# B, C and x of a state space mixer: from 256-channel to 512-channel products, with PE transposes behind them

## The chip, the cores and the metric

The kernel runs on one core of a Trainium2 chip. The metric is device time in microseconds (us): 1674.48 us is the median of three runs of the kernel before (1671.82 to 1675.09). TensorE (PE) does matmuls, VectorE (DVE) and ScalarE (ACT) work element by element, GpSimd (POOL) does almost nothing here, and SyncE (SP) issues the loads. PE writes to PSUM, of which this kernel uses two pools of four one-bank tiles each.

## The reference, cut to what matters

One encoder block: 256 tokens of width 2048 are normed, multiplied by one wide input matrix, and the columns are given to two mixers side by side (a Mamba-2 state space mixer, SSD, and an RWKV-7 mixer). Their outputs go through one output matrix, and a gated feed-forward part follows. All is float32. The change touches the columns `xbc` of the state space mixer:

```python
u = rms_norm(h, norm1_g[l])
P = u @ w_in[l]                       # 256 x 11744
xbc = P[..., o1:o2]                   # 2048 columns x, 512 columns B, 512 columns C
xbc = jax.nn.silu(causal_depthwise_conv(xbc, conv_w, conv_b))   # 4 taps along the tokens, per channel
xs = xbc[..., :D_SSD]
Bm = xbc[..., D_SSD:D_SSD + 512].reshape(b, s, 4, 128)          # four groups
Cm = xbc[..., D_SSD + 512:].reshape(b, s, 4, 128)
```

The convolution runs along the tokens and has its own weights for each channel.

## The kernel before

**Products.** Every matrix of weights comes from memory as "raw" tiles of 128 partitions x 1024 float32 (512 KB). `split` (L189) makes two halves of each: `whi`, rounded by ACT (L192), and `wlo = raw - whi`, by DVE (L193). The activations are kept split in the same way (`uh`, `ul`). Each product is the sum of three matmuls: high x high, high x low, low x high. One raw tile, with its two halves, is called a unit here. There are four buffers each for `raw`, `whi` and `wlo`, so a raw tile is loaded when the `wlo` of the unit four before it has been made, and a `whi` is made when PE has done with the unit four before it.

There are two forms of product:

- `gemm_a` (L267) puts channels on the partitions: the weights are the stationary operand (128 x 128), and the 256 tokens stream past. It makes 256 channels in one PSUM tile with 16 x 2 x 3 = 96 matmuls of 256 columns, 24 to a unit. The norm's factor of each token then lies along the columns, and `scaled` (L229, its instruction is L231) multiplies it in on DVE.
- `gemm_b` (L284) puts tokens on the partitions: the activations are stationary (two halves of 128 tokens), and 512 columns of weights stream past. It makes 512 channels in two PSUM tiles with 16 x 2 x 3 = 96 matmuls of 512 columns, 12 to a unit. The norm's factor of a token is then one number per partition, which an ACT instruction can take as its scale.

**The state space mixer.** B and C (L934 to L944): four `gemm_a` of 256 channels, each followed by `scaled` and two `conv`. A `conv` (L928) of 128 channels is one ACT instruction (L930) and three DVE instructions (L932) that read the product from PSUM; it needs channels on the partitions, since its weights are per channel. One Silu over all of B and C ends it. Then, for each of the four groups g (L1054 on): first a part of the output product of the RWKV mixer (g = 0 and 1); two `gemm_a` of 256 channels for x, each with `scaled`, two `conv` and a Silu into `xc`; for g = 2 and 3 a part of the output product of this mixer (`add_out`, which calls `gemm_b`); then the gate z as one `gemm_b`, with two ACT instructions that take it out of PSUM (L1072); then the group's scan as ten steps (`ssd_group`).

**What sets the order.** Small work is interleaved with the products by hand: `Side` (L42) is a queue of functions with due times in ticks, and the products call `side.tick(0.5)`; a unit is one tick in either form. The tail of the RWKV mixer (a chain of small dependent steps) is spread over the B and C products in this way, and its last pair over group 0; the scan of group g over the products behind it. A scheduler then orders each engine's instructions by a simulation, with the order of the program as priority; it also gives tiles their buffers. All loads are issued by SP in one queue.

Of the kernel before, what the change touches and what calls it, by code (L numbers as in the profile page):

```python
# [10 lines left out]
F32 = mybir.dt.float32  # L11
F32R = mybir.dt.float32r
AF = mybir.ActivationFunctionType
# [3 lines left out]
P = 128  # L17
T = 256
D = 2048
KT = D // P  # L20
D_FF = 5632
CXBC = 2048
# [46 lines left out]
def tile_hybrid_block(ctx: ExitStack, tc: tile.TileContext, x, norm1_g, w_in, conv_w, conv_b, dt_bias, A_log, D_skip,  # L69
                      ssd_norm_g, mu, w0, w2, a0, a2, g2, k_k, k_a, r_k, gn_w, gn_b, w_out, norm2_g, w_gate, w_up,  # L70
                      w_down, norm_f_g, out):
    nc = tc.nc
    PS = bass.MemoryType.PSUM
    x = x[0]
    out = out[0]
    w_in, conv_w, w2, a2, g2 = w_in[0], conv_w[0], w2[0], a2[0], g2[0]
# [4 lines left out]
    wpool = ctx.enter_context(tc.tile_pool(name="wpool", bufs=3))  # L81
# [4 lines left out]
    side = Side()  # L86

    def mmt(name):
        return mm.tile([P, 2, T], F32, name=name, tag="mm")

    def mxt(name):
        return mx.tile([P, 512], F32, name=name, tag="mx")
# [7 lines left out]
    ident = const.tile([P, P], F32, name="ident")  # L100
# [13 lines left out]
    ps = mxt("ps_up")  # L114
# [9 lines left out]
    rows = [init.tile([P, P], F32, name=f"rows{i}") for i in range(3)]  # L124
# [27 lines left out]
    for hh in range(2):  # L152
        for s in range(2):
            m = mask2[hh * 64:(hh + 1) * 64, s]
# [4 lines left out]
    for s in range(2):  # L159
        for hh in range(2):  # L160
            a = hh * 64
# [20 lines left out]
    ps = mxt("ps_cols")  # L182
# [13 lines left out]
    uh = ul = R = None  # L196
    ssq = [const.tile([P, 2, 4], F32, name=f"ssq{i}") for i in range(3)]
    rstd = [const.tile([P, 2], F32, name=f"rstd{i}") for i in range(3)]
# [30 lines left out]
    def scaled(ps):  # L229

        nc.vector.tensor_tensor(ps, ps, R.unsqueeze(1).broadcast_to([P, 2, T]), ALU.mult)  # L231
        return ps
# [34 lines left out]
    def gemm_a(w, cols, name, units=None):  # L267
        ps = mmt(name)
        for k0 in range(0, KT, 4):
            hi, lo = split(load_a(w, cols, k0)) if units is None else units(k0 // 4)  # L270
            for k in range(4):
                kt = k0 + k
                first, last = kt == 0, kt == KT - 1
                for b in range(2):
                    o = ps[:, b]
                    wh, wl = hi[:, k, b * P:(b + 1) * P], lo[:, k, b * P:(b + 1) * P]
                    nc.tensor.matmul(o, wh, uh[:, kt], start=first and b == 0, stop=False)  # L277
                    nc.tensor.matmul(o, wh, ul[:, kt], start=False, stop=False)  # L278
                    nc.tensor.matmul(o, wl, uh[:, kt], start=False, stop=last and b == 1)  # L279
                if k % 2:  # L280
                    side.tick(0.5)
        return ps

    def gemm_b(w, r0, c0, acts, name, turned=False):  # L284


        ps = [mmt(name).rearrange("p a t -> p (a t)") for _ in range(2)]
        n = len(acts)
        wv = w[r0:r0 + n * P, c0:c0 + 512].rearrange("(k p) c -> p k c", p=P)
        for k0 in range(0, n, 2):  # L290
            raw = wpool.tile([P, 2, 512], F32, name="raw", tag="raw", bufs=4)
            if turned:
                nc.sync.dma_start(out=raw[:, 0], in_=wv[:, k0])
                for a in range(2):
                    nc.sync.dma_start(out=raw[a * 64:a * 64 + 64, 1], in_=wv[64 - a * 64:P - a * 64, k0 + 1])
            else:
                nc.sync.dma_start(out=raw, in_=wv[:, k0:k0 + 2])
            hi, lo = split(raw)
            for k in range(2):
                kt = k0 + k  # L300
                first, last = kt == 0, kt == n - 1
                ah, al = acts[kt]
                for b in range(2):
                    s = slice(b * P, (b + 1) * P)
                    nc.tensor.matmul(ps[b], ah[:, s], hi[:, k], start=first, stop=False)  # L305
                    nc.tensor.matmul(ps[b], ah[:, s], lo[:, k], start=False, stop=False)  # L306
                    nc.tensor.matmul(ps[b], al[:, s], hi[:, k], start=False, stop=last)  # L307
                side.tick(0.5)
        return ps

    def add_out(w, r0, ys, then=None, turned=False, ns=range(4)):

# [30 lines left out]
    for r, c in ((rows[1], colB), (rows[0], colA), (rows[2], colC)):  # L343
        ps = mxt("ps_cols")
# [27 lines left out]
    pst = ExitStack()  # L372
    pp = pst.enter_context(tc.tile_pool(name="pp", bufs=1, side="right"))

    ps = scaled(ps_l0)
# [4 lines left out]
    ps = scaled(gemm_a(w_in, [(0, 96, CWD), (96, 32, CDT), (128, 128, CAD)], "ps_l1"))  # L380
# [501 lines left out]
    def window(pi, ticks):  # L882
        if pi < 8:
            w = pairs[pi]
            w["load"]()
            for t, n in zip(PREP, ("decay", "rate", "keys", "keys2", "keysum", "btt", "vt", "ktt")):
                side.at(t, w[n])
        if 0 < pi < 9:
            w = pairs[pi - 1]
            for t, f in zip(AMATS, w["amats"]):  # L890
                side.at(t, f)
            for t, f in zip(INV, w["inv"]):
                side.at(t if ticks >= 16 else t * (ticks - 0.5) / 16, f)
        if pi > 1:
            for t, f in zip(CHAIN, pairs[pi - 2]["chain"]):
                side.at(t if ticks >= 16 else t * (ticks - 0.5) / 16, f)
# [11 lines left out]
    for pi in range(8):  # L908
# [3 lines left out]
        for i, (n, c) in enumerate((("k", CK), ("v", CV), ("r", CR))):  # L912
            ps = scaled(gemm_a(w_in, [(0, 256, c + pi * 256)], "ps_rkv"))
            t = pp.tile([P, 2, T], F32, name="rkv", tag="t" + n, bufs=1)
            for j in range(2):
                m = ((c - CR) // P) + 2 * pi + j
# [9 lines left out]
    xzst = ExitStack()  # L926

    def conv(dst, ps, blk):  # L928
        w = [colC[:, 24 * j + blk:24 * j + blk + 1] for j in range(4)]
        nc.scalar.activation(dst, ps, AF.Identity, bias=colB[:, CB + blk:CB + blk + 1], scale=w[3])  # L930
        for s in range(1, 4):
            nc.vector.scalar_tensor_tensor(dst[:, s:], ps[:, :T - s], w[3 - s], dst[:, s:], ALU.mult, ALU.add)  # L932

    for i in range(4):  # L934
        ps = scaled(gemm_a(w_in, [(0, 256, CXBC + 2048 + i * 256)], "ps_bc"))
        if i == 0:
            pst.close()
            bcp = xzst.enter_context(tc.tile_pool(name="bcp", bufs=1, side="right"))
            xz = xzst.enter_context(tc.tile_pool(name="xz", bufs=2, side="right"))
            BC = bcp.tile([P, 2, 4, T], F32, name="BC")  # L940
        for j in range(2):
            b = 2 * i + j
            conv(BC[:, b // 4, b % 4], ps[:, j], 16 + b)
    nc.scalar.activation(BC, BC, AF.Silu)  # L944
    side.drain()
    window(9, 18)

    def ssd_group(g, xc, zs):
        st = {}

        def tl(name, shape, bufs=1, tag=None):
            return sp.tile(list(shape), F32, name=name, tag=tag or name, bufs=bufs)
# [16 lines left out]
        def cbt():  # L969
            ps = mxt("ps_cb").rearrange("p (a t) -> p a t", a=4)  # L970
            for c in range(2):
                s = slice(c * P, (c + 1) * P)
                nc.tensor.matmul(ps[:, c], BC[:, 0, g, s], BC[:, 1, g, s], start=True, stop=True)
            nc.tensor.transpose(out=ps[:, 2], in_=BC[:, 0, g, 0:P], identity=ident)
            cb = tl("cb", (P, 2, P))
# [43 lines left out]
        def off():  # L1019
            ec = tl("ec", (P, 8))  # L1020
            nc.scalar.activation(ec, cs[:, 1, hs], AF.Exp)
            ps = mxt("ps_of").rearrange("p (e v) -> p e v", e=8)
            nc.tensor.matmul(ps, BC[:, 1, g, P:T], st["sv"], start=True, stop=True)
            t = tl("xs", (P, 8, 64))
# [29 lines left out]
    for g in range(4):  # L1054
        xc = []
        if g == 0:
            out_rwkv(2, (2, 3))
        elif g == 1:
            out_rwkv(3, (0, 1, 2, 3))
        for i in range(2):  # L1060
            ps = scaled(gemm_a(w_in, [(0, 256, CXBC + g * 512 + i * 256)], "ps_xs"))
            t = xz.tile([P, 2, T], F32, name="xc", tag=f"xc{i}")
            for j in range(2):
                conv(t[:, j], ps[:, j], 4 * g + 2 * i + j)
            nc.scalar.activation(t, t, AF.Silu)
            xc.append(t)
        if g >= 2:
            add_out(w_out, (g - 2) * 512, [yq.popleft() for _ in range(2)])
        psz = gemm_b(w_in, 0, g * 512, uacts, "ps_z")
        zs = xz.tile([P, 2, 512], F32, name="zs")  # L1070
        for b in range(2):
            nc.scalar.activation(zs[:, b], psz[b], AF.Silu, scale=rstd[0][:, b:b + 1])  # L1072
        side.drain()
        if g == 0:
            est.close()
            est = ExitStack()
            sp = est.enter_context(tc.tile_pool(name="sp", bufs=1))
        for t, f in zip(SSD, ssd_group(g, xc, zs)):
            side.at(t if g < 3 else t / 3, f)
# [36 lines left out]
    for j in range(D_FF // 512):  # L1116
        c = j * 512
# [18 lines left out]
    for n in range(4):  # L1136
        raw = wpool.tile([P, 2, 512], F32, name="raw", tag="raw", bufs=4)
# [8 lines left out]
    for b in range(2):  # L1146
        s = slice(b * P, (b + 1) * P)
        for n, (hi, lo) in enumerate(ws):
            ps = mmt("ps_f").rearrange("p a t -> p (a t)")
# [4 lines left out]
            c = slice(n * 512, (n + 1) * 512)  # L1154
# [6 lines left out]
    for b in range(2):  # L1161
        r = finish(2, b)
        for n in (2, 3, 0, 1):
            c = slice(n * 512, (n + 1) * 512)
            t = hg[b][n]
# [33 lines left out]
```

## Time and profile before

| | |
|---|---|
| median of three runs | 1674.48 us (1671.82 to 1675.09) |
| the profiled execution, its own time | 1671.13 us |
| its span in the profile | 1669.4 us |
| granted TensorE clock | 0.996 |
| bytes moved by DMA | 286.97 MB, mean 172 GB/s |
| instructions | 31147 |

The span runs from the first to the last instruction of the profiled execution; 1.7 us of that execution's time lie around it. B and C stand from about 527 to 586 us of the span, and the four groups from about 586 to 876 us (their x from 601 to 829 us, their z from 629 to 876 us). After that come the rest of the output product and the feed-forward part, which the change doesn't touch. A row of a timeline gives the start in us, the duration in us, the engine, the line, the operation, the tiles written and read, and in brackets the idle time before and what ended it. A PE matmul's duration includes its way through the array, which overlaps the next one: what a matmul costs in a stream is the distance from its start to the next one's start.

### The profile page before, as it was taken

What the parts mean: (1) busy time and instruction counts of PE and PEld (TensorE: products, weight loads), DVE (VectorE), ACT (ScalarE), POOL (GpSimd) and SP (SyncE); (2) the same over time, 40 slices, a digit from 0 to 9 for tenths busy, and PEclk for the clock granted to TensorE, in tenths of its full rate; (3) what the DMA queues carried; (4) which work ended last, traced back from release to release, by engine and by line L of the source; (5) the groups of instructions that cost most, each with busy time, mean ns of one, the idle gap of its engine ahead of it and who ended that gap; (6) DMA issues with size and microseconds to landing.
All of it is one profiled execution on the core that took longest, in us unless ns stands there. A gap on an engine that the chain in (4) does not pass through costs nothing.

```text
span 1669.4 us, 31147 instructions
## 1 busy us (share of the span) xinstructions
PE 1640.1 (98%) x12514; PEld 1422.7 (85%) x12514; DVE 1172.9 (70%) x1827; ACT 910.7 (55%) x1488; POOL 17.9 (1%) x57
## 2 busy tenths in 40 slices
PE   8999999999999999999999999999999999999997
PEld 8998898988888988998988888888888888888886
DVE  7887898788887867877778656465565564554657
ACT  6654775766755648657665544444444444444444
POOL 3000000000000000000000000000000000000000
PEclk9998999999999999999999999999999999999999
DMA  8653554454455556765655666666666666666663
GB/s 247 184 143 104 134 135 126 137 140 139 138 142 144 154 152 188 233 191 155 180 176 152 202 189 190 194 189 189 196 190 189 190 189 196 189 191 192 190 189 126
DMA packets 219473, 286.97 MB, mean 172 GB/s; under 512 B 41762, under 2 KB 124480, under 8 KB 218688
## 3 DMA queue, kind: packets, MB, share of 16 engines
q1 hardware_dynamic: 218000, 282.68, 58.1%
q8 instruction: 98, 1.61, 0.4%
q0 software_dynamic: 752, 1.24, 0.3%
q10 hardware_dynamic: 576, 1.05, 0.2%
q14 instruction: 47, 0.39, 0.1%
HBM read 281.75 MB, written 3.18 MB: 171 GB/s over the span
## 4 chain that ended last, share of the span: by engine, by line
PE 77%; DVE 9%; ACT 6%; issue 3%; DMA 3%; SPq 1%; DVEq 0%; POOL 0%; ACTq 0%
PE ps_o L305 8%; PE ps_o L306 8%; PE ps_o L307 8%; PE ps_gt L306 5%; PE ps_up L307 5%; PE ps_gt L305 5%; PE ps_up L306 5%; PE ps_gt L307 5%; PE ps_up L305 5%; DVE wlo L193 2%; PE ps_xs L277 2%; ACT whi L192 2%; PE ps_rkv L277 2%; PE ps_xs L278 2%; PE ps_xs L279 2%
## 5 line engine op out<-in xcount | busy, mean ns | idle before, releaser
L193 DVE TENSOR_TENSOR wlo<-raw,whi 128x1024 fp32r<-128x1024 f32 x508 | 619.9, 1222 | 376.9 <-ACT whi L192 375.8
L192 ACT CAST whi<-raw 128x1024 fp32r<-128x1024 f32 x508 | 532.7, 1051 | 596.8 <-PE ps_o L307 159.6
L277 PE MATMUL ps_rkv<-uh,whi 128*128 128x256 f32 x768 | 227.7, 296 | 0.0
L279 PE MATMUL ps_rkv<-uh,wlo 128*128 128x256 f32 x768 | 218.9, 285 | 0.0
L278 PE MATMUL ps_rkv<-ul,whi 128*128 128x256 f32 x768 | 218.8, 285 | 0.0
L277 PEld LDWEIGHTS ps_rkv<-uh,whi 128*128 128x128 f32 x768 | 147.5, 192 | 5.3 <-issue 0.7
L278 PEld LDWEIGHTS ps_rkv<-ul,whi 128*128 128x128 f32 x768 | 147.9, 193 | 1.2 <-issue 0.3
L279 PEld LDWEIGHTS ps_rkv<-uh,wlo 128*128 128x128 f32 x768 | 147.6, 192 | 0.4
L305 PE MATMUL ps_gt<-whi,uh 128*128 128x512 f32 x352 | 137.1, 389 | 0.0
L307 PE MATMUL ps_gt<-whi,ul 128*128 128x512 f32 x352 | 137.0, 389 | 0.0
L306 PE MATMUL ps_gt<-wlo,uh 128*128 128x512 f32 x352 | 136.9, 389 | 0.0
L305 PE MATMUL ps_up<-whi,uh 128*128 128x512 f32 x352 | 136.9, 389 | 0.0
L306 PE MATMUL ps_up<-wlo,uh 128*128 128x512 f32 x352 | 136.9, 389 | 0.0
L307 PE MATMUL ps_up<-whi,ul 128*128 128x512 f32 x352 | 136.9, 389 | 0.0
L305 PE MATMUL ps_o<-whi,ah 128*128 128x512 f32 x336 | 131.7, 392 | 0.0
L307 PE MATMUL ps_o<-whi,al 128*128 128x512 f32 x336 | 130.9, 390 | 0.0
L306 PE MATMUL ps_o<-wlo,ah 128*128 128x512 f32 x336 | 130.7, 389 | 0.0
L305 PE MATMUL ps_o<-whi,yh 128*128 128x512 f32 x256 | 105.6, 412 | 0.0
L307 PE MATMUL ps_o<-whi,yl 128*128 128x512 f32 x256 | 100.9, 394 | 0.0
L306 PE MATMUL ps_o<-wlo,yh 128*128 128x512 f32 x256 | 100.8, 394 | 0.0
L318 DVE TENSOR_TENSOR h<-ps_o,h 128x512 f32<-128x512 f32 x152 | 98.5, 682 | 1.7 <-PE ps_o L307 1.1
L306 PEld LDWEIGHTS ps_up<-wlo,uh 128*128 128x128 f32 x352 | 66.1, 188 | 13.7
(342 smaller groups left out, 2982.4 us busy)
## 6 DMA issues: line engine op xcount, KB each, us to landing
raw<-in_w_in_dram SPq DMA_DIRECT2D x180, 512.0 KB, 4.0
raw<-in_w_gate_dram SPq DMA_DIRECT2D x88, 512.0 KB, 3.7
raw<-in_w_up_dram SPq DMA_DIRECT2D x88, 512.0 KB, 3.7
raw<-in_w_down_dram SPq DMA_DIRECT2D x88, 512.0 KB, 4.6
raw<-in_w_out_dram SPq DMA_DIRECT2D x32, 512.0 KB, 4.0
raw<-in_w_out_dram SPq DMA_DIRECT2D x32, 256.0 KB, 4.2
raw<-in_w_out_dram SPq DMA_DIRECT2D x64, 128.0 KB, 4.0
csb<-cs_d SPq DMA_DIRECT2D x4, 1024.0 KB, 6.5
```

The source lines that it names most:

```text
L192: order(nc.scalar.copy(hi, raw))
L193: order(nc.vector.tensor_tensor(lo, raw, hi.bitcast(F32), ALU.subtract))
L277: nc.tensor.matmul(o, wh, uh[:, kt], start=first and b == 0, stop=False)
L278: nc.tensor.matmul(o, wh, ul[:, kt], start=False, stop=False)
L279: nc.tensor.matmul(o, wl, uh[:, kt], start=False, stop=last and b == 1)
L305: nc.tensor.matmul(ps[b], ah[:, s], hi[:, k], start=first, stop=False)
L306: nc.tensor.matmul(ps[b], ah[:, s], lo[:, k], start=False, stop=False)
L307: nc.tensor.matmul(ps[b], al[:, s], hi[:, k], start=False, stop=last)
L318: nc.vector.tensor_tensor(d, ps[b], d, ALU.add)
```

## The change

B, C and, for each group, x become products of 512 columns in the `gemm_b` form (`rows_of`): six of them in place of twelve `gemm_a`. Two ACT instructions take such a product out of PSUM into a tile `rows_in` in SBUF, and multiply the norm's factor in. `rows_in` uses one of the four `raw` buffers. Later, as side work, `channels(i)` turns 256 of the 512 columns by four PE transposes of 128 x 128 into a tile of the other PSUM pool, and the `conv` instructions read that. For B this is done one tick into the product of C, both halves at once; for C one tick into the output product behind it (it is put into the queue after the drain and after `window(9, 18)`); for x at tick 1 and tick 1.5 of what follows it (the z product for g = 0 and 1, the output product for g = 2 and 3). The Silu over B and C is done once for B and once for C. `gemm_b` takes its column slice at another place, and can take two ranges of columns, which nothing here uses.

```diff
@@ gemm_b @@
-        wv = w[r0:r0 + n * P, c0:c0 + 512].rearrange("(k p) c -> p k c", p=P)
+        parts = [(0, 256, c0[0]), (256, 256, c0[1])] if isinstance(c0, tuple) else [(0, 512, c0)]
+        wv = w[r0:r0 + n * P].rearrange("(k p) c -> p k c", p=P)
...
-                nc.sync.dma_start(out=raw, in_=wv[:, k0:k0 + 2])
+                for at, m, c in parts:
+                    nc.sync.dma_start(out=raw[:, :, at:at + m], in_=wv[:, k0:k0 + 2, c:c + m])
...
+    def rows_of(c0, name):
+        ps = gemm_b(w_in, 0, c0, [(uh[:, k], ul[:, k]) for k in range(KT)], name)
+        rows = wpool.tile([P, 2, 512], F32, name="rows_in", tag="raw", bufs=4)
+        for b in range(2):
+            nc.scalar.activation(rows[:, b], ps[b], AF.Copy, scale=rstd[0][:, b:b + 1])
+
+        def channels(i):
+            ps = mxt("ps_tr").rearrange("p (j t) -> p j t", j=2)
+            for j in range(2):
+                for b in range(2):
+                    c = i * 256 + j * P
+                    nc.tensor.transpose(out=ps[:, j, b * P:(b + 1) * P], in_=rows[:, b, c:c + P], identity=ident)
+            return ps
+
+        return channels
@@ B and C @@
-    for i in range(4):
-        ps = scaled(gemm_a(w_in, [(0, 256, CXBC + 2048 + i * 256)], "ps_bc"))
-        if i == 0:
-            pst.close()
-            bcp = xzst.enter_context(tc.tile_pool(name="bcp", bufs=1, side="right"))
-            xz = xzst.enter_context(tc.tile_pool(name="xz", bufs=2, side="right"))
-            BC = bcp.tile([P, 2, 4, T], F32, name="BC")
-        for j in range(2):
-            b = 2 * i + j
-            conv(BC[:, b // 4, b % 4], ps[:, j], 16 + b)
-    nc.scalar.activation(BC, BC, AF.Silu)
+    def conv_bc(f, i):
+        for m in range(2):
+            ps = f(m)
+            for j in range(2):
+                b = 2 * m + j
+                conv(BC[:, i, b], ps[:, j], 16 + 4 * i + b)
+        nc.scalar.activation(BC[:, i], BC[:, i], AF.Silu)
+
+    turn_b = rows_of(CXBC + 2048, "ps_bc")
+    pst.close()
+    bcp = xzst.enter_context(tc.tile_pool(name="bcp", bufs=1, side="right"))
+    xz = xzst.enter_context(tc.tile_pool(name="xz", bufs=2, side="right"))
+    BC = bcp.tile([P, 2, 4, T], F32, name="BC")
+    side.at(1, lambda: conv_bc(turn_b, 0))
+    turn_c = rows_of(CXBC + 2560, "ps_bc")
     side.drain()
     window(9, 18)
+    side.at(1, lambda: conv_bc(turn_c, 1))
@@ each group g @@
-        for i in range(2):
-            ps = scaled(gemm_a(w_in, [(0, 256, CXBC + g * 512 + i * 256)], "ps_xs"))
+        turn_x = rows_of(CXBC + g * 512, "ps_xs")
+
+        def conv_x(i, f=turn_x, g=g, xc=xc):
             t = xz.tile([P, 2, T], F32, name="xc", tag=f"xc{i}")
+            ps = f(i)
             for j in range(2):
                 conv(t[:, j], ps[:, j], 4 * g + 2 * i + j)
             nc.scalar.activation(t, t, AF.Silu)
             xc.append(t)
+
+        side.at(1, lambda f=conv_x: f(0))
+        side.at(1.5, lambda f=conv_x: f(1))
```

More of the change, by code (lines that the diff above doesn't have):

```diff
@@ L292, in gemm_b @@
             if turned:
-                nc.sync.dma_start(out=raw[:, 0], in_=wv[:, k0])
+                nc.sync.dma_start(out=raw[:, 0], in_=wv[:, k0, c0:c0 + 512])
                 for a in range(2):
-                    nc.sync.dma_start(out=raw[a * 64:a * 64 + 64, 1], in_=wv[64 - a * 64:P - a * 64, k0 + 1])
-            else:
-                nc.sync.dma_start(out=raw, in_=wv[:, k0:k0 + 2])
+                    nc.sync.dma_start(out=raw[a * 64:a * 64 + 64, 1],
+                                      in_=wv[64 - a * 64:P - a * 64, k0 + 1, c0:c0 + 512])
+            else:
+                for at, m, c in parts:
+                    nc.sync.dma_start(out=raw[:, :, at:at + m], in_=wv[:, k0:k0 + 2, c:c + m])
             hi, lo = split(raw)
```

## The prediction

> **What bounds the kernel now.** First the page: the span, the busy times, the chain that ended last, the two halves of the split, the loads.
>
> ```profile
> span 1669.4 us, 31147 instructions
> PE 1640.1 (98%) x12514; PEld 1422.7 (85%) x12514; DVE 1172.9 (70%) x1827; ACT 910.7 (55%) x1488; POOL 17.9 (1%) x57
> PE 77%; DVE 9%; ACT 6%; issue 3%; DMA 3%; SPq 1%; DVEq 0%; POOL 0%; ACTq 0%
> L193 DVE TENSOR_TENSOR wlo<-raw,whi 128x1024 fp32r<-128x1024 f32 x508 | 619.9, 1222 | 376.9 <-ACT whi L192 375.8
> L192 ACT CAST whi<-raw 128x1024 fp32r<-128x1024 f32 x508 | 532.7, 1051 | 596.8 <-PE ps_o L307 159.6
> raw<-in_w_in_dram SPq DMA_DIRECT2D x180, 512.0 KB, 4.0
> ```
>
> PE is busy nearly all the time and holds 77% of the chain, and ACT's casts wait for PE to give back a `whi`: the supply runs ahead. An average over stages doesn't show that for the stages of the change, so the windows come next: first the B and C products, then the start of group 0, then the rest of groups 0 and 1, then groups 2 and 3.
>
> ```profile
> 527.00:566.00 39.00, 38.27 (x572) 35.98 (x572) 30.35 (x65) 20.40 (x52) 0.00 (x0) 1.00 0.47 126
> 566.00:601.00 35.00, 35.00 (x313) 30.43 (x313) 27.28 (x42) 20.22 (x32) 0.00 (x0) 1.00 0.58 168
> 601.00:727.00 126.00, 125.71 (x888) 111.13 (x887) 93.87 (x162) 82.21 (x134) 0.00 (x0) 1.00 0.66 199
> 727.00:876.00 149.00, 149.00 (x885) 131.31 (x884) 111.66 (x179) 97.58 (x127) 0.00 (x0) 1.00 0.57 171
> ```
>
> The columns are the length, then busy time of PE, weight loads, DVE, ACT and POOL, then the clock (1.00, full) and DMA. PE lacks 0.73 + 0.29 = 1.0 us of 349. So little can be won by removing waits; the change is worth what it does to the PE stream itself. How far ahead the supply is, one unit at the border from z of group 1 to x of group 2 shows (timelines of ACT, DVE, PE and SP):
>
> ```profile
> 719.46 1.05 ACT L192 CAST whi<-raw 128x1024 fp32r<-128x1024 f32 x1 [1.20 <-PE ps_z L307]
> 720.54 1.23 DVE L193 TENSOR_TENSOR wlo<-raw,whi 128x1024 fp32r<-128x1024 f32 x1 [1.03 <-ACT whi L192]
> 727.42 0.28 PE L277 MATMUL ps_xs<-uh,whi 128*128 128x256 f32 x1
> 727.65 0.28 PE L279 MATMUL ps_xs<-uh,wlo 128*128 128x256 f32 x1
> 710.35 1.23 DVE L193 TENSOR_TENSOR wlo<-raw,whi 128x1024 fp32r<-128x1024 f32 x1 [0.48 <-ACT whi L192]
> 711.61 19.29 SPq L264 DMA_DIRECT2D raw<-in_w_in_dram  x8
> ```
>
> `wlo` of that unit is done at 721.77 and first used at 727.65: 5.9 us early. Its load was issued at 711.61, just when the `wlo` of the unit four before it ended (710.35 + 1.23 = 711.58); with 4.0 us to land it is there at 715.6, 3.9 us before its cast. These two covers, 5.9 and 3.9 us, hide whatever I cost at nothing below.
>
> **The change part by part.** *Matmuls.* The counts of what goes, and the ACT and DVE work around it:
>
> ```profile
> L277 PE MATMUL ps_bc<-uh,whi x128: 278/283/467, 527.3 to 585.4; 128*128 128x256 f32 x128
> L231 DVE TENSOR_TENSOR ps_bc<-ps_bc,R x4: 693/696/700, 545.6 to 586.0; 128x512 f32<-128x512 f32 x4
> L277 PE MATMUL ps_xs<-uh,whi x256: 277/283/682, 600.6 to 827.6; 128*128 128x256 f32 x128
> L932 DVE SCALAR_TENSOR_TENSOR xc<-ps_xs,colC,xc x48: 441/476/486, 617.9 to 835.8; 128x255 f32<-128x255 f32 x16, 128x254 f32<-128x254 f32 x16, 128x253 f32<-128x253 f32 x16
> L930 ACT ACTIVATE xc<-ps_xs,colB,colC x16: 542/560/568, 616.6 to 833.1; 128x256 f32<-128x256 f32 x16
> L231 DVE TENSOR_TENSOR ps_xs<-ps_xs,R x8: 691/699/700, 615.8 to 828.2; 128x512 f32<-128x512 f32 x8
> L1072 ACT ACTIVATE zs<-ps_z,rstd x8: 681/688/691, 654.5 to 876.5; 128x512 f32<-128x512 f32 x8
> ```
>
> L278 and L279 have as many as L277, so 3 x (128 + 256) = 1152 matmuls of 256 columns go, and 576 of 512 columns come. The duration shown (283 ns) is not the price, since matmuls overlap; starts are. A unit of x runs undisturbed from the first row here to the second, and four units of z from the third to the fourth:
>
> ```profile
> 685.49 0.28 PE L279 MATMUL ps_xs<-uh,wlo 128*128 128x256 f32 x1
> 688.37 0.28 PE L279 MATMUL ps_xs<-uh,wlo 128*128 128x256 f32 x1
> 714.04 0.39 PE L306 MATMUL ps_z<-wlo,uh 128*128 128x512 f32 x1
> 724.92 0.39 PE L306 MATMUL ps_z<-wlo,uh 128*128 128x512 f32 x1
> ```
>
> 24 matmuls in 2.88 us are 0.120 us each; 4 x 12 in 10.88 us are 0.2267 us each. Twice the columns cost 0.2267 and not 0.240: each matmul has some 0.013 us that don't depend on its columns. 1152 x 0.120 = 138.2 us go and 576 x 0.2267 = 130.6 us come: **-7.7 us**, all of it on PE, which sets the end. The Trainium skill ("TensorE: Matmul & The Clock Gate", Back-to-back issue gap) gives a warm matmul N/2.4 + 2.5 ns, by which the fixed part would be 2.5 ns and this term -1.4 us. The two distances above disagree with that here, and I go by them.
>
> *Transposes.* Eight for each of six products, 48 in all. The feed-forward part has the same operation in a stream of 512-column matmuls:
>
> ```profile
> 979.01 0.39 PE L307 MATMUL ps_gt<-whi,ul 128*128 128x512 f32 x1
> 979.24 1.03 PE L1109 MATMUL ps_t<-ident,gt 128*128 128x128 f32 x8
> 980.03 0.48 PE L305 MATMUL ps_gt<-whi,uh 128*128 128x512 f32 x1
> 980.35 0.40 PE L306 MATMUL ps_gt<-wlo,uh 128*128 128x512 f32 x1
> ```
>
> Eight take 0.79 us from start to the next matmul's start (0.099 each), and that matmul takes 0.32 where 0.227 is usual: 0.09 more for each interruption. B and C: 2 x (0.79 + 0.09) = 1.8 us. x: eight interruptions of four, 8 x (0.40 + 0.09) = 3.9 us. Together **+5.7 us** on PE. From below, a transpose can't be under its share of columns, 128/512 x 0.2267 = 0.057, which makes 48 x 0.057 = 2.7 us.
>
> *Exits.* Twelve L231 of 0.70 leave DVE (-8.4 us); twelve ACT instructions like L1072, 0.688 each, come (+8.3 us). ACT is busy 52 to 66% of these windows and DVE 74 to 78%, and both ends lie under the 5.9 us of cover: nothing. The new ACT pair waits for the product's last matmul; queued behind it stand the next casts, which would be waiting for PE to free a `whi` anyway, as in the row at 719.46. The z products end in just such a pair already.
>
> *The turn.* PE meets the transposes one tick, 12 x 0.2267 = 2.7 us, after the product's end. By then ACT must have done the pair, perhaps behind one cast: 1.05 + 2 x 0.69 = 2.4 us. That fits by 0.3 us; if it fails by 1 us six times, it costs 6 us, for behind the transposes the whole PE stream waits. I take nothing. The conversions come in larger lots: 12 DVE instructions of 0.48 (5.8 us) for B, for C, and for the two halves of x within half a tick. The cover of 5.9 us just holds that, and the scheduler can put a `wlo` between them. The transposed tiles hold a buffer of the small PSUM pool for two `conv`, some 4 us, which the RWKV tail uses too; C's conversion moves behind the drain and the last window, whose loads keep their place in SP's queue, since it issues none. Nothing for these.
>
> *Loads.* As many, as large, in 2 KB pieces instead of 1 KB. The one place of four that `rows_in` takes in the ring of raw buffers is the first rival.
>
> *Group 0.* Here the cover is already gone:
>
> ```profile
> 638.75 0.39 PE L305 MATMUL ps_z<-whi,uh 128*128 128x512 f32 x1
> 639.41 0.50 PE L306 MATMUL ps_z<-wlo,uh 128*128 128x512 f32 x1 [0.27 <-DVE wlo L193]
> 628.43 0.69 DVE L847 TENSOR_TENSOR ysq<-vt,bon 128x512 f32<-128x512 f32 x1 [2.83 <-ACT ysq L833]
> 628.30 1.03 ACT L192 CAST whi<-raw 128x1024 fp32r<-128x1024 f32 x1
> 635.51 2.95 ACT L192 CAST whi<-raw 128x1024 fp32r<-128x1024 f32 x3
> 638.17 3.46 DVE L193 TENSOR_TENSOR wlo<-raw,whi 128x1024 fp32r<-128x1024 f32 x3
> ```
>
> While the RWKV tail ends, ACT makes no `whi` from 629.33 to 635.51, and PE then waits for `wlo`. One half of x is converted here now; with the change both are. ACT gets 2 x 0.69 + 2 x 0.56 = 2.5 us more, DVE 6 x 0.48 - 0.70 = 2.2 us more, all in these ten us. Between nothing (the conversions can wait until the casts are through: xc is needed only after z) and 4 us (both lists in a row, less what fits in gaps) I take **+1.0 us**, nearer to the small wait that the row shows.
>
> Sum: -7.7 + 5.7 + 1.0 = **-1.0 us**. Against the profiled execution that is 1671.13 - 1.0 = 1670.1 us (span 1668.4). The median of the runs lies 3.35 us above that execution, so against the median it is 1673.5 us. A measurement of this kernel can tell some 0.2%, 3.35 us, from no change: I forecast no change that can be measured, since two terms of 8 and 6 us nearly cancel.
>
> **The rivals.** *The raw ring runs dry (slower).* If `rows_in` keeps its buffer from its turn in the ring until the second transposes, the fourth load behind each product is issued only then. For x: tick 1.5 is 4.1 us into the next product, plus 0.49 of transposes, 4.0 to land, 1.05 and 1.22 to split: 10.9 us, where PE wants it after three units, 8.2 us. 2.7 us late, four times; for B and C, at tick 1 with eight transposes, 2.7 + 0.9 + 6.3 = 9.9, late by 1.7, twice. +14.2 us, 1674.48 - 2.0 + 14.2 = 1686.7 us. It decides when the buffer is taken well before the product ends. Against it: the loads for four units behind the product are out before its end (15.8 us lie between 711.61 and 727.42), so if the buffer is given only when the ACT pair writes it, a load later loses a unit of 2.7 us from its 3.9 us of cover, and nothing shows. For it: nothing in this profile shows which.
>
> *Group 0 takes its full price.* +4 in place of +1: 1676.5 us. For it the row at 639.41; against it that DVE waited 2.83 us for ACT just before, so there is room.
>
> *All falls well (faster).* Transposes at their lower bound, no price in group 0, and the 1.0 us of PE waits gone with DVE's 8.4 us: -7.7 + 2.7 - 1.0 = -6.0, 1668.5 us. Against it: 0.099 is measured at the same operation.
>
> *B and C don't give their share.* If the RWKV tail sets the pace from 527 to 586 us, two of six products save nothing, and -7.7 becomes -5.1: +1.6 us, 1676.1 us. Against it: PE is busy 38.27 of 39.00 us there.
>
> *Width saves nothing.* If a matmul's fixed part vanishes in the new stream, -7.7 becomes 0: +6.7, 1681.2 us. The skill's 2.5 ns would come near it (+5.3); both distances speak against it.
>
> **How the numbers follow.** Forecast 0.46, raw ring 0.09, full price in group 0 0.13, all well 0.22, B and C 0.07, width 0.03. Faster by over 0.2%: 0.22 and 0.04 of the forecast's tail, 0.26. Slower: 0.09 + 0.03, and 0.09 from the turns that come too late and from group 0 at its worst, 0.21. The rest, 0.53, is no change. The range takes in the faster rival and late transposes (+6 on the forecast): 1668.0 to 1680.0 us; the raw ring, the width rival and the outer tails stay out.
>
> **What would show it.** PE should have 576 - 1152 + 48 = 528 fewer matmuls; `ps_xs` and `ps_bc` matmuls 0.227 apart; eight transposes in 0.79 us and four in 0.4, each with a next matmul of 0.32; DVE 8.4 us less busy, ACT 8.3 us more. Gaps of PE ahead of a transpose put down to `rows_in` would show the turn coming too soon; gaps at `wlo` around 640 us, group 0; casts that wait for the raw load, three or four units behind a product, the ring. I am wrong if the windows of these stages shrink or grow by more than some 3 us, or if PE's distances aren't those above.

## The result: 1.5% slower, and the profile after

The changed kernel takes 1698.57 us (median of four runs, 1695.49 to 1700.72); the kernel before, run beside it, takes 1673.15 us (four runs, 1668.65 to 1675.09). The ratio is 1.0153, with a 95% interval of 1.0131 to 1.0175: some 25 us lost, where the forecast was 1.0 us won. The profiled execution of after took 1699.31 us, 28.2 us more than that of before. Single executions of one kernel spread by several us; in the traces a stretch at half clock near 126 us of the span, long before the change, lasts longer in some than in others (last section).

The page of after, in the lines that answer to those shown of before:

```profile
span 1697.6 us, 30069 instructions
PE 1649.1 (97%) x11986; PEld 1398.8 (82%) x11986; DVE 1163.5 (69%) x1815; ACT 912.8 (54%) x1497; POOL 17.8 (1%) x57
PE 74%; DVE 10%; ACT 7%; issue 3%; DMA 3%; SPq 2%; DVEq 0%; ACTq 0%
L193 DVE TENSOR_TENSOR wlo<-raw,whi 128x1024 fp32r<-128x1024 f32 x508 | 619.1, 1221 | 388.1 <-ACT whi L192 384.8
L192 ACT CAST whi<-raw 128x1024 fp32r<-128x1024 f32 x508 | 532.5, 1051 | 586.7 <-PE ps_o L310 168.6
raw<-in_w_in_dram SPq DMA_DIRECT2D x180, 512.0 KB, 4.3
```

The 528 matmuls fewer are there (12514 to 11986). The casts are as many and as long, a load lands in 4.3 us where it was 4.0, and no engine but PE is nearer to its limit. On the whole page only PE's share of the chain (77% to 74%) hints at trouble. The windows by stage say more. First before, cut where the same work starts and ends (B and C; groups 0 and 1; groups 2 and 3), then after:

```profile
527.31:600.63 73.32, 72.59 (x879) 65.80 (x873) 56.95 (x105) 40.05 (x83) 0.00 (x0) 1.00 0.52 147
600.63:727.42 126.79, 126.50 (x896) 111.84 (x890) 94.45 (x162) 83.00 (x134) 0.00 (x0) 1.00 0.66 199
727.42:876.10 148.68, 148.68 (x883) 131.03 (x882) 111.45 (x178) 97.26 (x127) 0.00 (x0) 1.00 0.57 170
```

```profile
526.75:603.72 76.97, 74.38 (x729) 57.09 (x725) 53.34 (x102) 42.49 (x88) 0.00 (x0) 1.00 0.46 130
603.72:742.96 139.24, 130.14 (x686) 103.44 (x685) 91.41 (x157) 85.92 (x137) 0.00 (x0) 0.98 0.60 186
742.96:904.27 161.31, 153.92 (x708) 125.50 (x706) 108.67 (x174) 94.20 (x127) 0.00 (x0) 0.97 0.51 156
```

The stages are 3.65, 12.45 and 12.63 us longer, 28.7 together; less the 0.56 us by which after enters them earlier, that is the whole loss of 28.2 us. Two columns show what it is made of. PE idles 19.1 us in the three rows (length less PE's busy time) where it idled 1.0. And the clock, the third column from the end, is no longer 1.00: in after's trace it stands at 0.50 for 3.41, 3.41, 3.41 and 6.83 us in these stages, 17.1 us, which costs about half of that, 8.5 us, of a busy PE. In before's trace it is at full there. The list of waits of after names one that the kernel before doesn't have:

```profile
ACT rows_in L320 <- PE ps_xs L310: 22.4, 3, 11.0
ACT rows_in L320 <- PE ps_bc L310: 7.1, 1, 7.1
```

ACT stood idle for 11.0 us before such a pair, and 29.5 us in four places, because it waited for the product to end. The timeline of ACT in after, at the end of x of group 2, shows what that means:

```profile
755.59 1.05 ACT L192 CAST whi<-raw 128x1024 fp32r<-128x1024 f32 x1 [0.64 <-ACT btok L1004]
767.64 1.31 ACT L320 ACTIVATE rows_in<-ps_xs,rstd 128x512 f32<-128x512 f32 x2 [10.99 <-PE ps_xs L310]
768.85 1.05 ACT L1013 ACTIVATE L<-L 128x1024 f32<-128x1024 f32 x1
769.79 0.58 ACT L1042 COPY sv<-ps_st 128x512 f32<-128x512 f32 x1
770.26 0.64 ACT L1060 ACTIVATE xs<-y 128x512 f32<-128x512 f32 x1
...
770.88 1.04 ACT L192 CAST whi<-raw 128x1024 fp32r<-128x1024 f32 x1
```

The cast at 755.59 is that of the product's last unit. The pair stands next in ACT's queue, and with it ACT waits for the end of the product. Only then, and behind small work of the scan that had queued up, comes the first cast of the next product. PE finds nothing made ahead, as its timeline shows:

```profile
771.98 0.73 PE L308 MATMUL ps_o<-whi,yh 128*128 128x512 f32 x2 [2.89 <-ACT whi L192]
773.23 0.50 PE L309 MATMUL ps_o<-wlo,yh 128*128 128x512 f32 x1 [0.52 <-DVE wlo L193]
```

Such waits for the `whi` or `wlo` of the first unit stand behind all six products and make some 11 of the 19.1 us. Most of the rest is in group 0. PE waits 1.7 us there for `rows_in` at two of the transposes, and 4.0 us at the first transposes of the scan, in the middle of z:

```profile
646.45 0.41 PE L990 MATMUL ps_xt<-ident,xc 128*128 128x128 f32 x2 [4.02 <-issue]
```

The row names no releaser, but they read x of group 0, and ACT's Silu over it ends at 646.35. A stretch at half clock follows, from 647.71.

It isn't the load. SP's timeline of after has three loads of the output matrix out well before:

```profile
752.37 5.97 SPq L300 DMA_DIRECT2D raw<-in_w_out_dram  x3
```

With the 4.3 us to land of the page's row above (3.8 to 4.0 for the output matrix), the first is there at 756.7, 11 us before the pair and 14 us before its cast. The fourth load is issued at 773.21, when the `wlo` of the first unit has been made, and PE shows no wait from 773.23 to 800 us: in that product it costs nothing. Beside it, ACT in before at the end of a z product, the place with which the prediction compared:

```profile
722.22 1.05 ACT L192 CAST whi<-raw 128x1024 fp32r<-128x1024 f32 x1 [1.71 <-PE ps_z L307]
724.90 1.06 ACT L192 CAST whi<-raw 128x1024 fp32r<-128x1024 f32 x1 [1.62 <-PE ps_z L307]
726.94 1.37 ACT L1072 ACTIVATE zs<-ps_z,rstd 128x512 f32<-128x512 f32 x2 [0.98 <-PE ps_z L307]
```

There the pair has casts of the next product ahead of it: these two and the one at 719.46. In after there is none ahead of the pair, at all six products.

### The profile page after: what moved, and what is told of

Same layout as the page of the kernel before. It is cut to its first block, busy times and chain, and to the rows that moved or that the text cites. A ratio compares the mean times of both kernels' runs of the same rounds, so it can differ in the third digit from the quotient of the medians.

```text
span 1697.6 us, 30069 instructions
## 1 busy us (share of the span) xinstructions
PE 1649.1 (97%) x11986; PEld 1398.8 (82%) x11986; DVE 1163.5 (69%) x1815; ACT 912.8 (54%) x1497; POOL 17.8 (1%) x57
## 4 chain that ended last, share of the span: by engine, by line
PE 74%; DVE 10%; ACT 7%; issue 3%; DMA 3%; SPq 2%; DVEq 0%; ACTq 0%
PE ps_o L308 8%; PE ps_o L309 7%; PE ps_o L310 7%; PE ps_up L309 5%; PE ps_gt L309 5%; PE ps_gt L310 5%; PE ps_gt L308 5%; PE ps_up L310 5%; PE ps_up L308 5%; DVE wlo L193 2%; PE ps_z L309 2%; ACT whi L192 2%; PE ps_rkv L277 2%; PE ps_z L310 2%; PE ps_xs L308 2%
## 5 line engine op out<-in xcount | busy, mean ns | idle before, releaser
L308 PEld LDWEIGHTS ps_up<-whi,uh 128*128 128x128 f32 x352 | 66.1, 188 | 13.8
```

## The experiments

The theory: it is the buffer in the ring. A tile from the ring is given in the order of the program, between the product's raw tiles and those of the next, and the scheduler then keeps the pair that writes it ahead of all casts behind it. The rivals: the fourth load behind each product, as the prediction priced it; the transposes or the turn itself; group 0.

**An own buffer.** `rows_in` gets one buffer of its own (the pools are opened earlier for that, and `zs` goes from two buffers to one to make room):

```diff
-        rows = wpool.tile([P, 2, 512], F32, name="rows_in", tag="raw", bufs=4)
+        rows = xz.tile([P, 2, 512], F32, name="rows_in", bufs=1)
...
-        zs = xz.tile([P, 2, 512], F32, name="zs")
+        zs = xz.tile([P, 2, 512], F32, name="zs", bufs=1)
```

> rows_in gets a buffer of its own for all six products (in the pool of xc, with one zs buffer instead of two to make room), all else as in the changed kernel. Ring theory (the raw ring held by rows_in costs the 28.2 us of span that the two profiles differ by): that difference goes, and the sum of matmuls and transposes is left, -2 to 0 us against before: 1671 to 1674 us. Rival (the ACT pair, the transposes and the larger lots of conversions cost it, whatever the buffer): still over 1690 us. Mixed: 1680 to 1690.

Measured: 1675.81 us against 1673.45 before, ratio 1.0017 (1.0001 to 1.0033). Some 23 us of the 25 are gone, though the time is 1.8 us above the range that was expected of the ring. ACT's timeline at the same place, the end of x of group 2:

```profile
756.18 1.05 ACT L192 CAST whi<-raw 128x1024 fp32r<-128x1024 f32 x1 [1.66 <-PE ps_xs L310]
758.90 1.05 ACT L192 CAST whi<-raw 128x1024 fp32r<-128x1024 f32 x1 [1.67 <-PE ps_xs L310]
761.58 1.04 ACT L192 CAST whi<-raw 128x1024 fp32r<-128x1024 f32 x1 [1.62 <-PE ps_xs L310]
765.45 1.38 ACT L320 ACTIVATE rows_in<-ps_xs,rstd 128x512 f32<-128x512 f32 x2 [2.83 <-PE ps_xs L310]
```

The same pair now has three casts of the next product ahead of it (two in group 0, three at the other products), and PE goes over the border without a wait. What is left is in group 0 (below).

**An own buffer for groups 1 to 3 alone.** B, C and group 0 stay in the ring:

```diff
+            xr = est.enter_context(tc.tile_pool(name="xr", bufs=1))
...
-        turn_x = rows_of(CXBC + g * 512, "ps_xs")
+        turn_x = rows_of(CXBC + g * 512, "ps_xs", xr)
```

> rows_in gets a buffer of its own for groups 1, 2 and 3 alone; B, C and group 0 still take theirs from the raw ring. In the changed kernel PE loses 5.2, 5.8 and 6.7 us against before around the x of these groups. Ring theory: these 17.7 us go and the steps at B, C and group 0 (11 us) stay: 1679 to 1683 us. Rival (exits, transposes, lots): within 4 us of the changed kernel's 1698.6 us.

Measured: 1682.6 us, ratio 1.0056 (1.0031 to 1.0080). In its trace B, C and group 0 have no cast ahead of the pair, groups 1 to 3 have three. Three products mended give back about 16 us of 25, the other three about 7: the cost goes with each product that uses the ring.

**The hole alone.** The kernel before with all its products, and only a tile taken from the ring behind the same six places, of which ACT writes and DVE later reads eight columns of each half:

```diff
+    def hole(ps, t):
+        rows = wpool.tile([P, 2, 512], F32, name="rows_in", tag="raw", bufs=4)
+        for b in range(2):
+            nc.scalar.copy(rows[:, b, 0:8], ps[:, b, 0:8])
+        side.at(t, lambda: nc.vector.tensor_copy(hole_to.rearrange("p (b c) -> p b c", b=2), rows[:, :, 0:8]))
...
```

> The kernel before, with its 256-channel products, and in it only the disturbance of the ring: at the six places a tile from the raw ring, in which ACT writes 8 columns of each half when the product has ended, and which DVE reads (8 columns of each half) at tick 1 or 1.5; nothing else uses it. Ring theory: 15 to 28 us slower than before, 1688 to 1701 us. Rival: within 3 us of before.

Measured: 1710.65 us (two runs), ratio 1.0218 (1.0184 to 1.0252). Nothing of the change is in it but this tile and its small copies, and it loses 37 us, more than the whole change and 9.7 us above the range that was expected. ACT's timeline at the end of x of group 2, and then PE's:

```profile
776.87 1.28 ACT L997 ACT_TABLE_LOAD   x1 [5.49 <-DVE L L995]
...
779.13 0.21 ACT L316 COPY rows_in<-ps_xs 128x8 f32<-128x8 f32 x2
...
782.87 1.98 ACT L192 CAST whi<-raw 128x1024 fp32r<-128x1024 f32 x2
```

```profile
783.38 0.87 PE L1050 MATMUL ps_yc<-ident,y 128*128 128x128 f32 x3 [5.69 <-DVE y L1047]
```

Behind two copies of 0.1 us the casts stand as they do behind the real pair: ACT idles 5.49 us ahead of them (here for a step of the scan) and no cast of the next product fills the gap. PE idles 24.3 us between 520 and 930 us, and the clock is at half for 30.7 us there. As at the real pair, no cast of the next product is ahead at any of the six places. Why it loses more than the whole change stays open; here the conversions that follow the product at once (L938) come ahead of the first cast as well.

**Converted at once.** As after, but the transposes and conversions come right behind each product, so that the ring's buffer is free at once:

```diff
-        side.at(1, lambda f=conv_x: f(0))
-        side.at(1.5, lambda f=conv_x: f(1))
+        conv_x(0)
+        conv_x(1)
...
```

> The changed kernel with transposes and conversions in the program right behind the product instead of a tick or more later; rows_in still in the raw ring. If the cost is the fourth load, which waits for the transposes: it is issued 1 to 1.5 units earlier, and the time falls by 1.7 to 2.7 us a product, 12 us or so, to about 1687 us. If the cost is that the ACT pair stands ahead of the next units' casts in ACT's order, so that PE begins the next product with nothing made ahead: within 4 us of 1698.6 us, or slower.

Measured: 1702.73 us (two runs), ratio 1.0171 (1.0138 to 1.0204), and the same 22.4 us of ACT waiting for `ps_xs` in three places. The edit moves the transposes clearly at groups 2 and 3 alone: the second ones come 1.5 us behind the product's last matmul here, 11.3 and 12.1 us in after, and the fourth load is issued 2.8 us earlier behind the product. The stage of these two groups takes 161.1 us, where it took 161.3 in after, so the earlier buffer brings nothing there: it is not the fourth load. At the other four products the transposes stand nearly as they did, and nothing is tested.

**The pair later.** As after, in the ring, but the tile is taken and the pair issued at tick 2 of the next product, the turn at tick 3 (x at 3 and 3.5):

```diff
...
+        side.at(2, take_x)
-        side.at(1, lambda f=conv_x: f(0))
-        side.at(1.5, lambda f=conv_x: f(1))
+        side.at(3, lambda f=conv_x: f(0))
+        side.at(3.5, lambda f=conv_x: f(1))
```

> The changed kernel, rows_in still in the raw ring, but the ACT pair and the tile stand in the program at tick 2 of what follows the product (the turn at 3, for x at 3 and 3.5), so that the loads and casts of two further units stand ahead of the pair. If the cost is the place of the pair ahead of the casts in ACT's order: the waits of PE at a product's first unit shrink by half or more, 1676 to 1688 us. If the cost is the buffer that is missing from the ring, it is missing here for as long: within 5 us of 1698.6 us.

Measured: 1677.40 us against 1672.98, ratio 1.0022 (1.0009 to 1.0036). The ring is used as before, and yet 22 us are back. ACT's timeline at the end of x of group 2:

```profile
746.69 1.05 ACT L192 CAST whi<-raw 128x1024 fp32r<-128x1024 f32 x1 [1.66 <-PE ps_xs L310]
749.41 1.05 ACT L192 CAST whi<-raw 128x1024 fp32r<-128x1024 f32 x1 [1.67 <-PE ps_xs L310]
755.95 1.37 ACT L323 ACTIVATE rows_in<-ps_xs,rstd 128x512 f32<-128x512 f32 x2 [5.49 <-PE ps_xs L310]
```

Two casts of the next product go ahead, at all six products. So what costs is the pair's place in ACT's queue; that a raw buffer is missing for a while costs little beside it (see the last experiment). The turn and the conversions move by two ticks with the pair here, and the wait of 4.0 us in group 0 is gone too, so not all of the 22 us need be the pair's own.

**Group 0 as before**, with the own buffer of the first experiment: x of group 0 by `gemm_a` and converted at once.

```diff
+        if g == 0:
+            turn_x = lambda i: scaled(gemm_a(w_in, [(0, 256, CXBC + i * 256)], "ps_xs"))
+        else:
+            turn_x = rows_of(CXBC + g * 512, "ps_xs")
...
```

> rows_in in a buffer of its own, as in the first experiment, and x of group 0 as in the kernel before (two products of 256 channels, converted at once). PE lost 4.0 us of waits and one stretch of half clock (1.7 us) in group 0 of the first experiment. If that is the crowding of group 0 by the end of the RWKV tail, they go and the rest of the sum (5 products: -6.4 of matmuls, +4.7 of transposes) is left: 1671 to 1673 us, 0.1% below before or no difference. If not: 1675 us or more.

Measured: 1670.65 us against 1672.98, ratio 0.9986 (0.9974 to 0.9999). That is 5 us under the first experiment, and the waits there are the place. PE in the first experiment, in z of group 0:

```profile
646.87 0.50 PE L309 MATMUL ps_z<-wlo,uh 128*128 128x512 f32 x1 [2.15 <-DVE wlo L193]
651.81 0.33 PE L990 MATMUL ps_xt<-ident,xc 128*128 128x128 f32 x1 [1.89 <-ACT xc L1093]
652.93 0.63 PE L308 MATMUL ps_z<-whi,uh 128*128 128x512 f32 x1
```

4.0 us of waits, and the last row, 0.63 long where 0.39 is usual, begins 3.41 us at half clock (1.7 us more).

**Group 0 later**, with the own buffer: the new form for all groups, but group 0's conversions at ticks 4 and 5.

```diff
-        side.at(1, lambda f=conv_x: f(0))
-        side.at(1.5, lambda f=conv_x: f(1))
+        side.at(1 if g else 4, lambda f=conv_x: f(0))
+        side.at(1.5 if g else 5, lambda f=conv_x: f(1))
```

> As the first experiment, with the conversions of x of group 0 at ticks 4 and 5 instead of 1 and 1.5. If the waits of group 0 come from conversions that fall among the last steps of the RWKV tail: the wait for wlo goes, and 1671 to 1674 us are left. If the ACT pair alone crowds it, or if the scan then waits for xc: 1675 us or more.

Measured: 1670.61 us, ratio 0.9988 (0.9975 to 1.0001). This kernel has the whole change without the two losses, that of the ring and that of group 0; its windows, cut by the same work:

```profile
526.71:600.08 73.37, 72.47 (x701) 56.16 (x697) 52.75 (x99) 42.44 (x88) 0.00 (x0) 1.00 0.51 142
600.08:727.89 127.81, 126.64 (x720) 102.46 (x714) 91.95 (x159) 82.28 (x136) 0.00 (x0) 1.00 0.64 200
727.89:876.09 148.20, 148.20 (x708) 122.57 (x706) 108.29 (x174) 95.08 (x127) 0.00 (x0) 1.00 0.57 170
```

349.38 us in all against before's 348.79: 2.1 us of waits where before has 1.0, no half clock, and no gain. PE's busy time in them is 0.46 us less.

**The transposes twice**, with the own buffer: each set of four is done twice, into the same place (the second overwrites the first with the same values).

```diff
...
+            for _ in range(2):
...
```

> As the first experiment, with every set of four transposes done twice over (the second writes the same result to the same place). By the price from the feed-forward part (0.099 us each in a row): 48 x 0.099 = 4.8 us more than the first experiment, 1679 to 1682 us. By the duration of one (0.27 us): 13 us more, 1688 us.

Measured: 1678.81 us, ratio 1.0032 (1.0016 to 1.0048), 3.0 us over the first experiment. The runs of both kernels spread over more than 10 us, so the sign fits and the size says little. Two things in the traces say more. In groups 2 and 3 (cut as in the windows above), where PE waits neither here nor in the first experiment, 16 transposes more make the stage 149.95 us long instead of 148.19: 0.11 us each, near the forecast's 0.099 and far from 0.27. And the price can be read from the starts in the trace of the seventh experiment (group 0 later):

```profile
707.89 0.60 PE L327 MATMUL ps_tr<-ident,rows_in 128*128 128x128 f32 x4
708.25 0.47 PE L308 MATMUL ps_z<-whi,uh 128*128 128x512 f32 x1
708.56 0.39 PE L309 MATMUL ps_z<-wlo,uh 128*128 128x512 f32 x1
...
761.42 1.04 PE L327 MATMUL ps_tr<-ident,rows_in 128*128 128x128 f32 x8
762.21 0.47 PE L309 MATMUL ps_o<-wlo,yh 128*128 128x512 f32 x1
762.52 0.39 PE L310 MATMUL ps_o<-whi,yl 128*128 128x512 f32 x1
```

Eight take 0.79 us from start to next start, four 0.36, and the matmul behind them 0.31 where 0.23 is usual.

**A control.** The kernel before with one buffer for `zs`, since the experiments with the own buffer had to take that:

```diff
-        zs = xz.tile([P, 2, 512], F32, name="zs")
+        zs = xz.tile([P, 2, 512], F32, name="zs", bufs=1)
```

> The kernel before with one zs buffer instead of two, the side edit that made room for rows_in in the first experiment. All theories: no difference from before, within 2 us. If it is slower or faster by more, the first, sixth and seventh experiments have to be read against it.

Measured: 1672.83 us against 1672.43, ratio 1.0006 (0.9989 to 1.0023). No difference that can be told.

**The pair later, and group 0 later too**, all in the ring:

```diff
...
+        side.at(2, take_x)
+        side.at(3 if g else 4, lambda f=conv_x: f(0))
+        side.at(3.5 if g else 5, lambda f=conv_x: f(1))
```

> As the experiment with the ACT pair at tick 2 and rows_in in the raw ring, with the turn and conversions of x of group 0 at ticks 4 and 5 instead of 3 and 3.5. If the place of the pair and the crowding of group 0 were all, this is as the version with a buffer of its own and a late group 0: 1670 to 1673 us. If the missing ring buffer still costs something of its own: 1674 to 1678 us.

Measured: 1677.01 us, ratio 1.0024 (1.0006 to 1.0041). Unlike with the own buffer, group 0 brings nothing here. Against the same with an own buffer (0.9988) some 6 us stay with the ring, even with the pair in a better place. In this trace PE idles 4.6 us between 520 and 930 us (before: 1.0), and the clock is at half for 3.41 us behind a wait of 2.02 us that ends at 663.64; how the rest comes about stays open.

## Why the prediction was wrong, step by step

**The step that failed is the exits.** It said of the new ACT pair: "queued behind it stand the next casts, which would be waiting for PE to free a `whi` anyway". Waiting they would be, but for one unit at a time: PE frees a `whi` every 2.7 us all through the product, so three casts of the next product fit in before it ends. In after none comes ahead of the pair, and the step that was put at nothing costs some 11 us of waits for the first unit, and half clock behind them. The z products, named as the example, have exactly these casts ahead of their pair, as the rows of before at 722.22 and 724.90 show; two rows more of the timeline would have told. What the step took for granted was the order on ACT. With the pair later, and the ring still in use, 22 us of the 25 come back (the turn's later place has a part in that), and the ring's tile alone brings the loss to a kernel that has nothing else of the change (the hole alone).

**The ring** stood among the rivals with a chance of 0.09 and a price of 14.2 us by way of the fourth load. The suspect was right, the way was not. Shown: loads are early (752.37, for a cast at 770.88), freeing the buffer sooner changes nothing in groups 2 and 3 (converted at once), the pair's place does. Argued and not shown: why the scheduler puts the pair there. The likely reason is that the tile, since it comes from the ring, is given a buffer in the order of the program, ahead of the raw tiles of the next units; with an own buffer the pair lets two or three casts pass.

**The clock** was in no step. The stages are 28.7 us longer in the profiled execution. About 8.5 of them are the 17.1 us at half clock that came with PE's waits. The waits themselves are 18.1 us (19.1 less 1.0). That leaves some 2 us, among them the small terms below and PE's ends ahead of waits, which count as busy; it isn't split further.

**Group 0** was forecast at +1.0, with +4 as a rival. The rival was right in size: 4.0 us of waits in the first experiment and 1.7 for the clock, and 5 us back when its conversions are moved. What failed is a reason for the small price, "xc is needed only after z". In before the first transposes of the scan stand behind z of group 0 (at 655.65; z's last matmul starts at 652.70). In the first experiment PE has them in the middle of z and waits there (651.81, z goes on to 666.6), and so it does in after (646.45, z goes on to 664.0). With the conversions later they stand behind z again. Why the order on PE changes isn't shown.

**Matmuls and transposes** held. In the seventh experiment's rows matmuls of 512 columns are 0.23 us apart, eight transposes take 0.79 us and the matmul behind 0.08 more; the prediction had 0.2267, 0.79 and 0.09. In groups 2 and 3, where PE waits neither in before nor there, the stage shrinks by 0.48 us (148.68 to 148.20); the two terms give 0.6 for these two products (a third of 7.7, less 4 x 0.49). Their sum for all six, -2.0 us, was not resolved: PE's busy time falls by 0.46 us in all windows of that experiment, and its runs put the whole change at -2.0 us with an interval from -4.2 to +0.2 (ratio times 1672.98). "No change that can be measured" thus fits the change when the pair and group 0 are out of the way, and is wrong for the change as it was made.

**DVE, ACT and the turn.** DVE is 9.4 us less busy (forecast 8.4). ACT is 2.1 us busier and not 8.3: its table loads (the ACT_TABLE_LOAD rows) went from 46 to 42, 59.0 to 53.9 us, which the step didn't count. Neither sets the end. The turn fits with the own buffer, where PE doesn't wait for `rows_in`; in after it waits 1.9 us for it in three places, the sign that the prediction named. But the transposes aren't where the step had them: in groups 2 and 3 of the seventh experiment they come 8.3 us behind the product, not 2.7.

## What to carry to other kernels

A result that is put into a ring of buffers shared with a stream of loads can take a place in the stream's order, and the engine that writes it may then wait for a product's end ahead of work that would have kept the next product fed; give it a buffer of its own, or issue it two units later (here the first was better by some 6 us). When an instruction that waits is added to a queue, don't ask only whether those behind it could run now, but how many of them used to run before the event it waits for: the rows of the queue ahead of a similar instruction tell. And where an engine with a throttled clock is the bound, a wait costs more than its length.

## What the runs showed of the hardware that was not expected

PE's granted clock falls to half after waits of 2 to 3 us. Windows of after at two such waits, which end at 719.17 (2.44 us, the row further down) and 852.82 (2.89 us):

```profile
719.40:722.80 3.40, 3.20 (x8) 1.99 (x8) 3.40 (x6) 3.27 (x4) 0.00 (x0) 0.50 0.57 170
852.50:859.30 6.80, 6.45 (x16) 4.65 (x17) 4.24 (x5) 3.72 (x5) 0.00 (x0) 0.50 0.46 137
```

PE's timeline of after at the first of them:

```profile
719.17 1.05 PE L308 MATMUL ps_z<-whi,uh 128*128 128x512 f32 x2 [2.44 <-ACT whi L192]
...
721.46 0.63 PE L309 MATMUL ps_z<-wlo,uh 128*128 128x512 f32 x1
721.88 0.63 PE L310 MATMUL ps_z<-whi,ul 128*128 128x512 f32 x1
...
723.24 0.39 PE L308 MATMUL ps_z<-whi,uh 128*128 128x512 f32 x1
723.47 0.39 PE L309 MATMUL ps_z<-wlo,uh 128*128 128x512 f32 x1
```

Matmuls are 0.43 us apart while the clock is at half and 0.23 after it. All these stretches last 3.41 us or 6.83. The Trainium skill ("TensorE: Matmul & The Clock Gate", What's actually happening) tells of a free-running activity window of 3413 ns, and the lengths agree with one window and with two. The starts agree too: in after the stretches behind waits begin at 647.71, 719.39, 774.01 and 852.51 us, and their distances, 71.68, 54.62 and 78.50 us, are 21, 16 and 23 times 3.413. Its table of advice in the same page (Why this matters for your kernels) allows idle gaps up to about 3 us; here a gap of 2.44 us was enough, and the measurement decides.

The length of a gap alone doesn't decide it in these traces; how long PE idles within one such window fits them better. Three windows of the first experiment, the last of which ends where its stretch at half clock begins:

```profile
642.62:646.03 3.41, 2.09 (x11) 1.41 (x9) 3.39 (x8) 3.41 (x6) 0.00 (x0) 1.00 0.00 0
646.03:649.45 3.42, 2.58 (x11) 2.13 (x12) 3.15 (x7) 3.34 (x8) 0.00 (x0) 1.00 0.43 110
649.45:652.86 3.41, 1.52 (x8) 0.96 (x7) 3.28 (x5) 3.38 (x5) 0.00 (x0) 1.00 0.49 157
```

The gap of 2.15 us that ends at 646.87 lies over the first two, 1.32 and 0.84 us of idle time, and the clock stays full. The gap of 1.89 us that ends at 651.81 lies in the third, and half clock follows. In after 1.91 us of idle time in the window from 770.59 to 774.00 were enough, 1.87 from 640.89 to 644.30 were not. This isn't one limit for all work: in the hole alone, among short matmuls, 1.39 us from 565.55 to 568.96 were enough.

The stretch at half clock near 126 us, which every trace here has, lasts 10.24 us in the profiled execution of before, 6.83 in that of after, 23.89 in those of the first experiment and of the transposes twice. Nothing of the change runs there, so it is a part of the spread of single runs, and one profiled execution can be off by several us for it alone. What sets its length isn't shown.
